# A hybrid decoder layer on one core: products of ones at the start, modulation products two blocks sooner, and the first k/v products taken in fours of blocks

## The chip, the cores and the metric

The kernel runs on one core of a Trainium2 chip. The metric is the device time of one execution in microseconds (us), median of several runs; lower is better. TensorE (PE) does the matrix products, VectorE (DVE), ScalarE (ACT) and GpSimd (POOL) the elementwise work, and SyncE (SP) issues most of the loads. Each engine takes its instructions in the order in which they are queued on it.

## The reference

One layer, 1024 positions by 1024 features, in float32. Only its start matters here:

```python
c_act = jax.nn.silu(c)
mod = c_act @ w_ada + b_ada                       # 6 x 1024 columns
sh1, sc1, g1, sh2, sc2, g2 = jnp.split(mod, 6, axis=-1)
h = rms_norm(x, pre_mix_g) * (1.0 + sc1) + sh1    # 1024 x 1024
proj = h @ w_in                                   # q, k, v and gates of two head groups
...                                               # mLSTM heads, windowed attention, w_out, gated MLP with convolution
```

## The kernel before

The positions are cut into 8 blocks of 128 (`b`), the features into 8 chunks of 128 (`k`), and most of the kernel works on transposed data: `xT[:, k, :]` holds chunk `k` of the normalized `x` for all positions. A product in float32 accuracy is made of three products of parts: each operand is split into a rounded part `hi` (a cast on ACT) and a remainder `lo` (a subtraction on DVE), and hi·hi, hi·lo and lo·hi are summed in PSUM.

**The front.** Everything from the first load to the end of the first projection stands inside `tc.manual_schedule()` (line 201), so that each engine there keeps the order in which the code is written; a planner orders most of what comes behind. The front has these steps:

- SP loads, in this order: the eight blocks of `x` (512 KB each), between them the constants and the first columns of `w_ada` (`ada_pair`, 512 KB a tile), then halves of the first two weight units (`first_load`), then more of `w_ada`.
- For each block, `x_square` (ACT, sum of squares), `rstd_of` (POOL, two small instructions), then `x_turn` (line 265): DVE scales the block by its reciprocal norm, and PE transposes it in eight 128x128 pieces into two PSUM banks, half 0 (tag `mm`, two buffers) and half 1 (tag `B`, two buffers). `x_evac(b, h, ...)` copies a bank into `xT`, on ACT (`C_`) or DVE (`D_`).
- The row of `c` is spread over all partitions by eight products with a slice of the identity (`cb`, line 305), which stand ahead of the first transposes on PE.
- Modulation of chunk 0 comes from PE: `ada_product(8)` and `ada_product(0)` are eight products each with a one-column moving operand (line 320). They stand on PE behind the transposes of block 5 and of block 6. Modulation of the other chunks comes from DVE: `ada_sum` (line 168) multiplies a 128x1024 tile by `cb` and sums it, two of them to a chunk; `shift_gain` makes the shift and the gain from the two sums.
- `h_part(k, t)` returns the four steps that make chunk `k` of `h` for half `t` of the positions (blocks 4t to 4t+3): the affine step on ACT [0] or on DVE [1], the cast to `hi` on ACT [2], the remainder `lo` on DVE [3]. `first_split(u, i)` returns the same two steps, cast and remainder, for half `i` of weight unit `u`.
- The first projection (line 418) runs over the chunks; in each, 16 accumulators (8 blocks, for k/v of attention, `kv`, and for half of the mLSTM values, `v`) take three products of 256 columns, 384 in all. `h_chunk(k)` issues the work for chunk `k + 1` ahead of chunk `k`'s products.

Behind line 334, before the change, the order on the engines is: affine step, cast, remainder of `h` chunk 0, first half, with the split of unit 0 between; the copies of blocks 6 and 7; the split of unit 1; the second half of `h` chunk 0; and then both sums of chunk 1.

Of the kernel before, what the change touches and what calls it, by code (L numbers as in the profile page):

```python
# [18 lines left out]
P = 128  # L19
D = 1024  # L20
S = 1024
NB = S // P
KD = D // P
# [34 lines left out]
def layer_kernel(  # L58
# [18 lines left out]
    V, A, G, T = nc.vector, nc.scalar, nc.gpsimd, nc.tensor  # L77

    def f(ap):
        return ap.bitcast(F32)  # L80
# [7 lines left out]
    def mm3(ps, lh, ll, rh, rl, first, last):  # L88
        T.matmul(ps, lh, rh, start=first, stop=False)  # L89
        T.matmul(ps, lh, rl, start=False, stop=False)  # L90
        return T.matmul(ps, ll, rh, start=False, stop=last)  # L91

    def rstd_of(dst, ssq, n):
        G.tensor_scalar(dst, ssq, 1.0 / n, EPS, op0=ALU.mult, op1=ALU.add)  # L94
        G.tensor_tensor(dst, dst, neghalf[:, : dst.shape[1]], op=ALU.pow)
# [7 lines left out]
    ones = cp.tile([P, P], F32, name="ones")  # L103
# [22 lines left out]
    pC = lambda name: py.tile([P, 512], F32, tag="C", bufs=2, name=name)  # L126
# [4 lines left out]
    def transposed_pair(i, name):  # L131
        return tuple(hp.tile([P, KD, 512], F32R, tag=f"{part}{i}", name=f"{name}{part}{i}") for part in ("hi", "lo"))
# [30 lines left out]
    def ada_load(j, w):  # L163
        nc.sync.dma_start(w, w_ada[j * P : (j + 1) * P, :])
        return w

    def ada_sum(j, w):
        return V.scalar_tensor_tensor(w, w, 0.5, cb, op0=ALU.mult, op1=ALU.mult, accum_out=mod[:, j : j + 1])  # L168
# [19 lines left out]
    units = []  # L188
# [14 lines left out]
    hT = [transposed_pair(i, "hT") for i in range(2)]  # L203
# [5 lines left out]
    def x_load(b):  # L209
        nc.sync.dma_start(xs[b], x[b * P : (b + 1) * P, :])  # L210

    def ada_tile(i, j):
        i = i if i < 10 else (i - 10) ^ 1
        if i < 2:
            return ap0.tile([P, D], F32, tag=f"w{i}", name=f"ada{j}")
        return block_tile(i - 2, f"ada{j}")[:, :D]
# [3 lines left out]
    def ada_pair(k, which=(0, 1)):  # L220
        for i in which:
            j = (8 + k, k)[i]
            adas[j] = ada_load(j, ada_tile(2 * k + i, j))
# [3 lines left out]
    def first_load(u, i):  # L227
        if len(first) <= u:
            raw = w_raw(f"w{u}raw")
            units.append(w_pair(f"w{u}"))  # L230
            first.append((raw, *units[u]))
        c = slice(512 * i, 512 * (i + 1))
        nc.sync.dma_start(first[u][0][:, c], w_in[u][:, c])

    def first_split(u, i):
        raw, hi, lo = (t[:, 512 * i : 512 * (i + 1)] for t in first[u])
        return lambda: A.copy(hi, raw), lambda: V.tensor_tensor(lo, raw, f(hi), op=ALU.subtract)

    nc.scalar.dma_start(ch8, c.rearrange("o (k m) -> (o k) m", k=KD))
    nc.scalar.dma_start(cc8, ccol)  # L240
    x_load(0)
# [3 lines left out]
    nc.sync.dma_start(cv, cols)  # L245
    ada_pair(0, (0,))
    x_load(6)
    x_load(7)
    ada_pair(0, (1,))
    first_load(0, 0)  # L250
    first_load(1, 0)
    ada_pair(1)
# [6 lines left out]
    def x_square(b):  # L259
        A.activation(hT[1][1][:, 6:8, :], xs[b].rearrange("p (a b) -> p a b", a=2), AF.Square, accum_out=ssq[:, b : b + 1])  # L260
        rstd_of(rst[:, b : b + 1], ssq[:, b : b + 1], D)
# [3 lines left out]
    def x_turn(b):  # L265
        V.tensor_scalar(xs[b], xs[b], rst[:, b : b + 1], None, op0=ALU.mult)
        for h in range(2):
            ps = xps[b, h] = (mm, pB)[h](f"xtp{b}")
            for i in range(4):
                T.transpose(ps[:, i * P : (i + 1) * P], xs[b][:, (4 * h + i) * P : (4 * h + i + 1) * P], ident)  # L270

    def x_evac(b, h, copy):
        copy(xT[:, 4 * h : 4 * h + 4, b * P : (b + 1) * P], xps[b, h].rearrange("p (a b) -> p a b", a=4))

    def shift_gain(k):
        c = slice(k, k + 1)
        V.tensor_tensor(mod[:, c], mod[:, c], cv[:, C_BADA + k : C_BADA + k + 1], op=ALU.add)
        V.scalar_tensor_tensor(g_mix[:, c], mod[:, 8 + k : 9 + k], cv[:, C_PREMIX + k : C_PREMIX + k + 1], gb[:, c], op0=ALU.mult, op1=ALU.add)

    def h_part(k, t):  # L280

        c = slice(k, k + 1)
        hk = xT[:, k, 512 * t : 512 * (t + 1)]
        hi, lo = (part[:, k, :] for part in hT[t])
        return (
            lambda: A.activation(hk, hk, AF.Identity, bias=mod[:, c], scale=g_mix[:, c]),
            lambda: V.tensor_scalar(hk, hk, g_mix[:, c], mod[:, c], op0=ALU.mult, op1=ALU.add),
            lambda: A.copy(hi, hk),
            lambda: V.tensor_tensor(lo, hk, f(hi), op=ALU.subtract),
        )  # L290

    C_, D_ = A.copy, V.tensor_copy
# [8 lines left out]
    for h in range(2):  # L301
        cbs.append((mm, pB)[h](f"cb{h}"))
        for i in range(4):
            k = 4 * h + i
# [10 lines left out]
    def ada_product(j):  # L315

        if not mps:
            mps.append(pA("mod0"))
        for k in range(KD):
            T.matmul(mps[0][:, j : j + 1], adas[j][:, k * P : (k + 1) * P], cc8[:, k : k + 1], start=k == 0, stop=k == KD - 1)  # L320

    for b in range(2, NB):
        x_turn(b)
        if b + 1 < NB:
            x_square(b + 1)
        x_evac(b - 2, 0, C_)
        x_evac(b - 1, 1, D_ if b < 6 else C_)
        if b == 5:

            V.scalar_tensor_tensor(gb, cv[:, C_BADA + 8 : C_BADA + 16], 1.0, cv[:, C_PREMIX : C_PREMIX + 8], op0=ALU.add, op1=ALU.mult)  # L330
            ada_product(8)
        if b == 6:
            ada_product(0)
    V.tensor_tensor(mod[:, 0:1], mps[0][:, 0:1], cv[:, C_BADA : C_BADA + 1], op=ALU.add)
    V.scalar_tensor_tensor(g_mix[:, 0:1], mps[0][:, 8:9], cv[:, C_PREMIX : C_PREMIX + 1], gb[:, 0:1], op0=ALU.mult, op1=ALU.add)
    h0, h1 = h_part(0, 0), h_part(0, 1)
    w0, w1 = first_split(0, 0), first_split(1, 0)
    h0[1]()
    w0[0]()
    h0[2]()  # L340
    w0[1]()
    h0[3]()
    x_evac(6, 0, C_)
    x_evac(7, 0, D_)
    w1[0]()
    w1[1]()
    h1[1]()
    h1[2]()
    h1[3]()
    x_evac(7, 1, C_)  # L350

    def ada_sums(k):
        for j in (8 + k, k):
            ada_sum(j, adas[j])
            yield
        shift_gain(k)

    for _ in ada_sums(1):
        pass

    def h_chunk(k):

        if k and k + 3 < KD:
            ada_pair(k + 3)
        sums = ada_sums(k + 2) if k + 2 < KD else iter(())
        if k + 1 < KD:
            for t in range(2):
                act, _, cast, rest = h_part(k + 1, t)
                act()
                cast()  # L370
                next(sums, None)
                rest()
        next(sums, None)
        if k == 0:
            for u in range(2):
                for do in first_split(u, 1):
                    do()
        ensure({1: 3, 3: 4}.get(k, 0))
# [32 lines left out]
    pkv = [p(f"kv{i}") for i in range(2) for p in (pA, pC)]  # L411
    pv = [p(f"v{i}") for i in range(2) for p in (mm, pB)]
    def passes(k):
        if k == 0:
            return [(n, b) for t in range(2) for n in range(2) for b in range(4 * t, 4 * t + 4)]
        return [(n, b) for n in ((0, 1) if k < KD - 1 else (1, 0)) for b in range(NB)]

    for k in range(KD):
        h_chunk(k)
        for n, b in passes(k):  # L420
                hi, lo = hT[b // 4]
                ts = slice((b % 4) * P, (b % 4 + 1) * P)
                uh, ul = (part[:, (k % 4) * 256 : (k % 4 + 1) * 256] for part in units[2 * (k // 4) + n])
                ps = (pkv, pv)[n][b // 2][:, 256 * (b % 2) : 256 * (b % 2 + 1)]

                mm3(ps, hi[:, k, ts], lo[:, k, ts], uh, ul, k == 0 and b % 2 == 0, k == KD - 1 and b % 2 == 1)
    V.tensor_scalar(nsink, rw[:, 8:16], -1.0, None, op0=ALU.mult)
    front.__exit__(None, None, None)
    ap0.release()
# [375 lines left out]
    for h in range(ML_H):  # L805
# [4 lines left out]
        k = conv_chunk(u, 4 + h, f"k{h}")  # L810
# [151 lines left out]
    for b in range(NB):  # L962
# [24 lines left out]
        ts = slice((b % 4) * P, (b % 4 + 1) * P)  # L987
        for h in range(2):
            ps = mm(f"ht{b}_{h}")
# [3 lines left out]
            for i in range(4):  # L993
                k = 4 * h + i
# [154 lines left out]
    units = [(i, r) for i in (1, 2, 6, 5, 7, 3, 4) for r in range(NP)]  # L1149
# [134 lines left out]
    for tb in range(4):  # L1284
        b = 4 + tb
# [101 lines left out]
```

## Time and profile before

| | |
|---|---|
| median of 3 runs | 1127.9 us (1127.55 to 1128.68) |
| the profiled execution | 1128.73 us, of which its span is 1126.7 |
| PE busy | 1110.8 us, 99% of the span, 5949 matmul instructions |
| DVE, ACT, POOL busy | 846.0, 563.2, 150.3 us |
| moved by DMA | 146.85 MB, 130 GB/s on average |

The span runs from the first to the last instruction of the profiled execution; the time holds 2.03 us more. Busy time of an engine is an average over stages, so the table says which engine carries the kernel and not what the first 40 us wait for. The profile also gives the TensorE clock that the chip granted, as a share of 2.4 GHz; its record begins with the first change of level, and what comes before that is shown as 1.00.

### The profile page before, as it was taken

What the parts mean: (1) busy time and instruction counts of PE and PEld (TensorE: products, weight loads), DVE (VectorE), ACT (ScalarE), POOL (GpSimd) and SP (SyncE); (2) the same over time, 40 slices, a digit from 0 to 9 for tenths busy, and PEclk for the clock granted to TensorE, in tenths of its full rate; (3) what the DMA queues carried; (4) which work ended last, traced back from release to release, by engine and by line L of the source; (5) the groups of instructions that cost most, each with busy time, mean ns of one, the idle gap of its engine ahead of it and who ended that gap; (6) DMA issues with size and microseconds to landing.
All of it is one profiled execution on the core that took longest, in us unless ns stands there. A gap on an engine that the chain in (4) does not pass through costs nothing.

```text
span 1126.7 us, 16175 instructions
## 1 busy us (share of the span) xinstructions
PE 1110.8 (99%) x5949; PEld 943.7 (84%) x5949; DVE 846.0 (75%) x1510; ACT 563.2 (50%) x1133; POOL 150.3 (13%) x227
## 2 busy tenths in 40 slices
PE   7999999999999999999999999999999999999997
PEld 6999998888899888877788888888888888888886
DVE  4946879857665456798897888879787877777686
ACT  6642534655535345575553545445454555454552
POOL 2012334554334100000000000000000000000021
PEclk8999999999999999999999999999999999999999
DMA  9625526242103222323333233233313359633445
GB/s 355 236 96 178 166 77 188 94 150 75 38 20 108 100 93 94 113 79 127 103 122 111 67 122 107 72 102 122 121 56 113 132 182 359 230 116 103 150 127 210
DMA packets 55166, 146.85 MB, mean 130 GB/s; under 512 B 5464, under 2 KB 5808, under 8 KB 55088
## 3 DMA queue, kind: packets, MB, share of 16 engines
q1 hardware_dynamic: 53056, 140.31, 37.2%
q10 hardware_dynamic: 2032, 5.51, 1.2%
q8 instruction: 47, 0.77, 0.3%
q14 instruction: 31, 0.25, 0.1%
HBM read 117.19 MB, written 28.61 MB: 129 GB/s over the span
## 4 chain that ended last, share of the span: by engine, by line
PE 90%; DVE 5%; ACT 2%; DMA 2%; issue 1%; POOL 0%; DVEq 0%; POOLq 0%; ACTq 0%
PE X L1036 7%; PE X L1035 7%; PE X L1037 7%; PE Y L1036 4%; PE Y L1037 4%; PE Y L1035 4%; PE dx L1217 3%; PE dx L1215 3%; PE dx L1216 3%; PE tg L89 3%; PE tg L90 3%; PE tg L91 3%; PE dz L1217 3%; PE dz L1216 3%; PE dz L1215 3%; PE y L89 3%
## 5 line engine op out<-in xcount | busy, mean ns | idle before, releaser
L94 POOL TENSOR_SCALAR rsb<-ssb 128x1 f32<-128x1 f32 x4 | 2.3, 576 | 606.8 <-ACT junk L1270 606.6
L1035 PE MATMUL X<-S,wl 128*128 128x512 f32 x156 | 62.5, 400 | 0.0
L1037 PE MATMUL X<-S,wl 128*128 128x512 f32 x156 | 61.7, 396 | 0.0
L1036 PE MATMUL X<-S,wl 128*128 128x512 f32 x156 | 61.6, 395 | 0.0
L1045 DVE SCALAR_TENSOR_TENSOR yg<-ug,cv,yg 128x1023 f32<-128x1023 f32 (+1 forms) x44 | 56.4, 1282 | 6.6 <-ACT yg L1042 6.6
L168 DVE SCALAR_TENSOR_TENSOR ada<-ada,cb 128x1024 f32<-128x1024 f32 x46 | 57.0, 1248 | 3.0 <-DMA ada<-in_w_ada_dram 3.0
L86 ACT CAST wl<-T 128x512 fp32r<-128x512 f32 x41 | 25.5, 622 | 66.1 <-PE X L1036 62.2
L1045 DVE SCALAR_TENSOR_TENSOR yv<-uv,cv,yv 128x1023 f32<-128x1023 f32 (+1 forms) x44 | 56.3, 1279 | 1.2 <-ACT yv L1042 1.2
L86 ACT CAST A<-ra 128x512 fp32r<-128x512 f32 x46 | 28.6, 621 | 49.4 <-PE dx L1217 20.1
L86 ACT CAST w<-T 128x512 fp32r<-128x512 f32 x47 | 29.1, 622 | 40.8 <-PE Z L1037 34.8
L1089 DVE TENSOR_TENSOR uv<-q,X 128x512 f32<-128x512 f32 x22 | 15.1, 687 | 41.3 <-PE X L1037 41.3
L86 DVE TENSOR_TENSOR w<-T,w 128x512 fp32r<-128x512 f32 x47 | 32.2, 689 | 15.4 <-ACT w L86 15.4
L86 DVE TENSOR_TENSOR A<-ra,A 128x512 fp32r<-128x512 f32 x46 | 31.8, 690 | 15.3 <-ACT A L86 15.3
L1217 PE MATMUL dx<-B,A 128*128 128x512 f32 x108 | 42.4, 393 | 0.0
L1216 PE MATMUL dx<-B,A 128*128 128x512 f32 x108 | 42.3, 391 | 0.0
L1215 PE MATMUL dx<-B,A 128*128 128x512 f32 x108 | 39.8, 394 | 0.0
L1037 PE MATMUL Y<-S,wl 128*128 128x512 f32 x92 | 36.4, 395 | 0.0
L1035 PE MATMUL Y<-S,wl 128*128 128x512 f32 x92 | 36.4, 395 | 0.0
L1036 PE MATMUL Y<-S,wl 128*128 128x512 f32 x92 | 36.4, 395 | 0.0
L86 ACT CAST wl<-fu 128x512 fp32r<-128x512 f32 x21 | 13.1, 622 | 46.3 <-PE Y L1036 43.4
L1036 PEld LDWEIGHTS X<-S,wl 128*128 128x128 f32 x156 | 29.3, 188 | 7.4 <-issue 0.5
L1035 PEld LDWEIGHTS X<-S,wl 128*128 128x128 f32 x156 | 29.3, 188 | 7.4 <-issue 0.5
(587 smaller groups left out, 3910.9 us busy)
## 6 DMA issues: line engine op xcount, KB each, us to landing
ada<-in_w_ada_dram SPq DMA_DIRECT2D x48, 512.0 KB, 4.2
ra<-a_dram SPq DMA_DIRECT2D x30, 512.0 KB, 3.9
fu<-in_w_up_dram SPq DMA_DIRECT2D x26, 512.0 KB, 3.5
a_dram<-yg SPq DMA_DIRECT2D x22, 512.0 KB, 3.7
rb<-in_w_down_dram SPq DMA_DIRECT2D x44, 256.0 KB, 4.4
fu_False<-in_w_up_dram SPq DMA_DIRECT2D x18, 512.0 KB, 3.5
a_dram<-s SPq DMA_DIRECT2D x11, 512.0 KB, 5.6
x<-in_x_dram SPq DMA_DIRECT2D x8, 512.0 KB, 7.5
```

Source lines behind the costliest of these rows:

```text
L86: return A.copy(hi, src), eng.tensor_tensor(lo, src, f(hi), op=ALU.subtract)
L89: T.matmul(ps, lh, rh, start=first, stop=False)
L90: T.matmul(ps, lh, rl, start=False, stop=False)
L91: return T.matmul(ps, ll, rh, start=False, stop=last)
L168: return V.scalar_tensor_tensor(w, w, 0.5, cb, op0=ALU.mult, op1=ALU.mult, accum_out=mod[:, j : j + 1])
L1035: T.matmul(ps, w[:, 0, ks], a[:, 0, k, :], start=st, stop=False, skip_group_check=True)
L1036: T.matmul(ps, w[:, 0, ks], a[:, 1, k, :], start=False, stop=False, skip_group_check=True)
L1037: ends = T.matmul(ps, w[:, 1, ks], a[:, 0, k, :], start=False, stop=en, skip_group_check=True)
L1045: V.scalar_tensor_tensor(t[:, sh:], src[:, : S - sh], w(tap), t[:, sh:], op0=ALU.mult, op1=ALU.add)
L1215: T.matmul(ps[tb], a[:, 0, ts], w[:, 0], start=first and r == 0, stop=False, skip_group_check=True)
L1216: T.matmul(ps[tb], a[:, 0, ts], w[:, 1], start=False, stop=False, skip_group_check=True)
L1217: ends = T.matmul(ps[tb], a[:, 1, ts], w[:, 0], start=False, stop=last and r == NP - 1, skip_group_check=True)
```

## The change

Five edits, all in the front:

1. Ahead of everything else, PE gets 12 products of the 128x128 tile `ones` with itself into a PSUM tile that nobody reads.
2. `ada_product(8)` moves from behind block 5's transposes to behind block 4's, `ada_product(0)` from behind block 6's to behind block 5's, and the load of the second one's weights goes ahead of the load of block 7.
3. The split of unit 0 moves into the loop over the blocks (iteration 6); the copy of block 6, half 1, moves out of the loop.
4. Behind the loop the order is new: one sum of chunk 1 stands between the two remainders of chunk 0 that it used to follow, the other ahead of the last remainder, and the copies of blocks 6 and 7 are all on ACT.
5. In the first projection, four accumulators at a time take their hi·hi products, then their hi·lo, then their lo·hi, where before each accumulator took its three in a row.

```diff
+    warm = pC("warm")
+    for i in range(12):
+        T.matmul(warm[:, :P], ones, ones, start=True, stop=True)
     nc.scalar.dma_start(ch8, c.rearrange("o (k m) -> (o k) m", k=KD))
...
     ada_pair(0, (0,))
     x_load(6)
+    ada_pair(0, (1,))
     x_load(7)
-    ada_pair(0, (1,))
     first_load(0, 0)
...
+    w0, w1 = first_split(0, 0), first_split(1, 0)
     for b in range(2, NB):
         x_turn(b)
         if b + 1 < NB:
             x_square(b + 1)
+        if b == NB - 2:
+            w0[0]()
+            w0[1]()
         x_evac(b - 2, 0, C_)
-        x_evac(b - 1, 1, D_ if b < 6 else C_)
+        if b < NB - 1:
+            x_evac(b - 1, 1, D_ if b < 6 else C_)
+        if b == 4:
+            V.scalar_tensor_tensor(gb, cv[:, C_BADA + 8 : C_BADA + 16], 1.0, cv[:, C_PREMIX : C_PREMIX + 8], op0=ALU.add, op1=ALU.mult)
+        if b == 4:
+            ada_product(8)
         if b == 5:
-            V.scalar_tensor_tensor(gb, cv[:, C_BADA + 8 : C_BADA + 16], 1.0, cv[:, C_PREMIX : C_PREMIX + 8], op0=ALU.add, op1=ALU.mult)
-            ada_product(8)
-        if b == 6:
             ada_product(0)
...
     h0, h1 = h_part(0, 0), h_part(0, 1)
-    w0, w1 = first_split(0, 0), first_split(1, 0)
-    h0[1]()
-    w0[0]()
-    h0[2]()
-    w0[1]()
-    h0[3]()
-    x_evac(6, 0, C_)
-    x_evac(7, 0, D_)
-    w1[0]()
-    w1[1]()
-    h1[1]()
-    h1[2]()
-    h1[3]()
-    x_evac(7, 1, C_)
...
-    for _ in ada_sums(1):
+    sums1 = ada_sums(1)
+    h0[1]()
+    h0[2]()
+    next(sums1)
+    h0[3]()
+    w1[0]()
+    w1[1]()
+    x_evac(6, 0, C_)
+    x_evac(7, 0, C_)
+    h1[1]()
+    x_evac(6, 1, C_)
+    h1[2]()
+    for _ in sums1:
         pass
+    h1[3]()
+    x_evac(7, 1, C_)
...
     for k in range(KD):
         h_chunk(k)
-        for n, b in passes(k):
-                hi, lo = hT[b // 4]
-                ts = slice((b % 4) * P, (b % 4 + 1) * P)
-                uh, ul = (part[:, (k % 4) * 256 : (k % 4 + 1) * 256] for part in units[2 * (k // 4) + n])
-                ps = (pkv, pv)[n][b // 2][:, 256 * (b % 2) : 256 * (b % 2 + 1)]
-                mm3(ps, hi[:, k, ts], lo[:, k, ts], uh, ul, k == 0 and b % 2 == 0, k == KD - 1 and b % 2 == 1)
+        todo = passes(k)
+        for i in range(0, len(todo), 4):
+            for term in range(3):
+                for n, b in todo[i : i + 4]:
+                    h_ = hT[b // 4][term == 2][:, k, (b % 4) * P : (b % 4 + 1) * P]
+                    w_ = units[2 * (k // 4) + n][term == 1][:, (k % 4) * 256 : (k % 4 + 1) * 256]
+                    ps = (pkv, pv)[n][b // 2][:, 256 * (b % 2) : 256 * (b % 2 + 1)]
+                    T.matmul(ps, h_, w_, start=k == 0 and term == 0 and b % 2 == 0, stop=k == KD - 1 and term == 2 and b % 2 == 1)
```

## Rows read from the trace of the kernel before

**Rows 1.** The page: busy time of the engines, granted clock in 40 slices.

```profile
PE 1110.8 (99%) x5949; PEld 943.7 (84%) x5949; DVE 846.0 (75%) x1510; ACT 563.2 (50%) x1133; POOL 150.3 (13%) x227
...
PEclk8999999999999999999999999999999999999999
```

**Rows 2.** Stretches (us): length, busy us and instructions by engine, clock, DMA share, GB/s.

```profile
10.10:15.40 5.30, 5.30 (x26) 4.96 (x26) 3.46 (x5) 5.30 (x13) 3.08 (x6) 1.00 1.03 412
...
18.80:22.20 3.40, 3.40 (x34) 3.40 (x32) 1.50 (x4) 1.79 (x5) 1.23 (x2) 1.00 1.04 418
22.20:26.40 4.20, 4.20 (x21) 3.96 (x21) 1.44 (x5) 1.55 (x4) 0.00 (x0) 0.51 0.99 391
26.40:29.10 2.70, 2.70 (x12) 2.46 (x12) 2.34 (x4) 1.23 (x3) 0.00 (x0) 0.50 1.01 395
29.10:33.60 4.50, 4.50 (x39) 4.45 (x38) 4.08 (x8) 1.61 (x3) 0.00 (x0) 1.00 1.00 401
...
200.00:1119.90 919.90, 918.78 (x4430) 761.40 (x4429) 696.56 (x1120) 465.95 (x896) 94.70 (x117) 1.00 0.35 118
```

**Rows 3.** Timeline of PE: start, duration, line, out<-in, count, idle before and releaser.

```profile
6.32 3.78 PE L305 MATMUL cb<-ch,ident 8*128 8x128 f32 x16 [6.32 <-DVE ch L296]
10.03 6.38 PE L270 MATMUL xtp<-ident,x 128*128 128x128 f32 x32
17.02 1.06 PE L270 MATMUL xtp<-ident,x 128*128 128x128 f32 x8 [0.61 <-DVE x L266]
...
19.18 1.84 PE L320 MATMUL mod<-cc,ada 128*128 128x1 f32 x16
...
21.79 2.96 PE L320 MATMUL mod<-cc,ada 128*128 128x1 f32 x16
24.61 1.95 PE L270 MATMUL xtp<-ident,x 128*128 128x128 f32 x8
26.42 0.58 PE L89 MATMUL kv<-w0hi,hThi 128*128 128x256 f32 x1
...
33.48 0.28 PE L91 MATMUL v<-w1hi,hTlo 128*128 128x256 f32 x1
34.34 0.38 PE L89 MATMUL kv<-w0hi,hThi 128*128 128x256 f32 x1 [0.59 <-ACT hThi L288]
...
37.04 0.28 PE L89 MATMUL kv<-w0hi,hThi 128*128 128x256 f32 x1
...
75.19 0.28 PE L89 MATMUL tg<-w4hi,hThi 128*128 128x264 f32 x1
```

**Rows 4.** The chain that ended last, 10 to 37 us, one piece of PE.

```profile
10.10 5.39 PE xtp L270 x24
```

**Rows 5.** Timeline of ACT in the front.

```profile
12.35 0.58 ACT L273 COPY xT<-xtp 128x512 f32<-128x512 f32 x1
...
17.68 1.06 ACT L260 ACTIVATE hTlo<-x 128x1024 fp32r<-128x1024 f32 x1
...
25.74 0.62 ACT L288 CAST hThi<-xT 128x512 fp32r<-128x512 f32 x1 [2.65 <-DVE xT L287]
```

**Rows 6.** Timeline of DVE in the front.

```profile
0.88 0.17 DVE L160 MEMSET ones<- 128x128 f32 x1 [0.88 <-PEq L1376]
...
15.52 0.69 DVE L273 COPY xT<-xtp 128x512 f32<-128x512 f32 x1 [0.42 <-PE xtp L270]
...
20.26 0.75 DVE L266 TENSOR_SCALAR x<-x,rst 128x1024 f32<-128x1024 f32 x1 [0.71 <-POOL rst L95]
24.79 0.16 DVE L334 TENSOR_TENSOR mod<-mod,cv 128x1 f32<-128x1 f32 x1 [3.77 <-PE mod L320]
...
30.09 1.22 DVE L168 SCALAR_TENSOR_TENSOR ada<-ada,cb 128x1024 f32<-128x1024 f32 x1
```

**Rows 7.** SP's issue of the load of `ada0`.

```profile
9.24 0.33 SPq L164 DMA_DIRECT2D ada<-in_w_ada_dram  x1
```

**Rows 8.** Loads issued from 9 to 10 us: size, us from issue to landing.

```profile
ada<-in_w_ada_dram SPq DMA_DIRECT2D x1, 512.0 KB, 9.4
```

## The prediction

> **What bounds the kernel now.** The page comes first: PE is busy for 99% of the span and every other engine for 75% or less [rows 1]. Stretches of the whole span then show where PE isn't: 1.1 us are lost between 200 and 1119.9 us [rows 2]. So behind the front there is no slack, and a front that hands over earlier should move the end by as much. What the front is worth is read from PE's timeline [rows 3]: the first k/v product starts at 26.42 us, the 384 of them end where the next unit's products start, at 75.19, and that is 48.8 us. Undisturbed they need less: the product at 37.04 is the 64th, so the last 321 take 38.15 us, 0.119 each, and 384 would take 45.6. Of the 3.15 us between, 1.5 lie in chunk 0 (48 products from 26.42 to 33.60, 7.2 us where 5.7 would do) and 1.65 in the first 15 products of chunk 1 (33.60 to 37.04). The first loss is the clock: from 22.2 to 29.1 us it was granted at about 0.5, the 1.2 GHz level, and 12 products took 2.7 us [rows 2]. The second is a wait for ACT [rows 3], and the chain behind it runs through DVE, where two sums of 1.22 us start at 30.09 [rows 6].
>
> So the time has two handles: K, the start of the first k/v product, and E, the excess over 45.6 us behind it. Before, K = 26.42 and E = 3.15.
>
> What sets K is PE's order. From 17.02 on PE has hardly a gap: blocks 4 and 5, product 8, block 6, product 0, block 7 [rows 3]. The clock matters here too. The granted level reads 1.00 until 22 us, but that is no measurement: 24 transposes from 10.10 on took 225 ns each [rows 4], eight from 17.02 on 133 ns with their tail [rows 3], so PE was at the low level until about 15.4. A block of eight transposes costs 1.8 us at the low level and 0.95 at the high one; a modulation product costs 1.8 to 3.0 us [rows 3]. PE was at the high level from 15.4, with blocks 3, 4 and 5; it then ran product 8, block 6 and the start of product 0, and at 22.2 the level had fallen.
>
> **The change part by part.** *Products of ones.* The tile is set at 1.05 us [rows 6], and PE had nothing before 6.32. Twelve products are 24 records like `cb`'s 16, which took 236 ns each [rows 3]: 5.7 us, so PE is free at 6.8 at worst, 0.4 late. If the level rises underway they end sooner, and `cb` takes 16 x 0.115 = 1.8 us (a record of a product at the high level) in place of 3.8. Either way this reaches K only in part: block 2 can't be transposed before block 0's bank is copied, and ACT does that at 12.35 to 12.93, behind its squares [rows 5]. PE would start block 2 at 12.9, where it started at 13.7 (10.10 and two blocks of 1.8). After 6.8 us PE has `cb` and two blocks with gaps between, so I take the low level at 12.9, as before.
>
> *Blocks 2 to 4.* Block 2 runs to 14.7. The level rises near 15.4, as before, and block 3 ends at 16.0. Block 4's scaling stands on DVE behind the copy of block 2's second half, which waited for PE at 15.52 before [rows 6] and now follows block 2: 14.7, 15.4, and 0.75 more is 16.15. Block 4 is done at 17.1, 1.0 earlier than before (17.02 + 1.06).
>
> *Products two blocks sooner.* Product 8 runs 17.1 to 18.9, block 5 to 19.9 or 20.7, product 0 to 21.6 (all high) or 23.6 (low from 18.9). Call this moment M; before it was 24.77. The mixture that preceded the fall, products with one column and few transposes, now starts at 17.1 in place of 19.2, so I expect the fall inside it, and take M = 22.8. Blocks 6 and 7 follow: 0.95 to 1.8 each. K is 23.5 (all high), 27.2 (all low), and 26.2 as the value taken, with both blocks mostly low.
>
> The loads trade places: `ada0`'s load was issued at 9.24 and landed 9.4 us later [rows 7, 8], so block 7 lands at 18.6. ACT squared it at 17.68 before [rows 5]; now at 18.7, one us later. Before, POOL's result and the scaling (20.26, 0.75 long) came 2.6 us behind the square's start [rows 5, 6], so block 7 is scaled at 22.0, and PE wants it no sooner than 22.5. That cover is gone only if K were below 23. The other loads keep their places.
>
> *Unit 0's split in the loop.* Cast and remainder, 0.6 and 0.7 us, leave the path between M and K. On DVE the remainder waits for the cast, the cast for ACT's square of block 7 until 19.8; the scaling of block 7 stands behind it and isn't due before 21.2. On ACT the copy of block 4's first half waits until 20.9 at latest, and block 6 needs that bank only at 21.6. I cost this at nothing.
>
> *Order behind M.* On DVE before, from 24.79 to the last of chunk 1's gain (32.7) there were 7.9 us. Now it is the gain (0.3), affine step (0.55), sum (1.22), two remainders (1.3), affine step (0.55), sum (1.22) and gain (0.2): 5.3 us. Chunk 1's first half is then ready on ACT (0.8 and a cast of 0.62 [rows 5]) at M + 6.8, and chunk 0's products don't end before K + 5.7, at least M + 7.6. The 1.65 us of chunk 1 vanish. New waits: the first `lo` is ready at M + 2.8, due eight products behind K, at M + 2.9 at the earliest; the second is ready at M + 6.1, due at M + 5.7 if K = M + 1.9, so at most 0.4 us. The copy of block 6, half 1, now ends at M + 3.6, when `v` of block 2 wants the bank.
>
> *Fours of blocks.* The same 384 products, each with its own weight load as before: PE and PEld count 5949 each [rows 1]. Before, a new accumulator began with every third product, at the same pace of 0.119, so the switch is free.
>
> **Sum.** E is 0.3 (three low products at 0.21 in place of 0.12) and 0.4 (the wait): 0.7. The last k/v product ends at 26.2 + 45.6 + 0.7 = 72.5, 2.7 us before 75.19. The profiled execution took 1128.73 us, 0.83 above the median; from its own time the sum is 1126.0, from the median 1125.2.
>
> **The rivals.** *High throughout*, the clock never falls after block 3. For it: PE has fewer gaps than before. Against: the same products preceded the fall at 22.2 [rows 2, 3]. K = 23.5, E = 0.4, end at 69.5: 1122.2.
>
> *Low into the k/v products*, the level returning 2.7 us behind K as it did before (26.42 to 29.1). For it: K comes behind few dense transposes. K = 27.2, E = 1.9, end at 74.7: 1127.4, no change.
>
> *Given back later*: something behind the front that follows a load or the planner's order keeps its time. Against: PE's 99%. It would read 1127.9.
>
> *Low from the first blocks to K*, the slower one. If the level never rises between 12.9 and K, blocks 2 to 4 end at 18.3, product 8 at 21.3, block 5 at 23.1, product 0 at 26.1, blocks 6 and 7 at 29.7. With E = 1.5 that ends at 76.8 (1129.5); with chunk 0 wholly low (48 x 0.094 = 4.5) at 79.8 (1132.5). It decides if the level hasn't risen by the end of block 4 (18.3) and doesn't rise in blocks 6 and 7 either. Against it stands what happened before: the level rose at 15.4 when PE had done nothing but transposes for 5.3 us [rows 2, 4]. The Trainium skill says otherwise (TensorE: Matmul & The Clock Gate, Part 4: PE-mode transpose): the full-speed clock doesn't engage for transposes, since they don't count as a busy PE. By that rule this rival would be the forecast, 1129.5 to 1132.5; the trace disagrees with it at 15.4, if these are that kind of transpose.
>
> **How the numbers follow.** A time within 0.2% (2.3 us) is what this kernel's measurement can't tell from no change. The likeliest case, a gain of 1.8 to 4.0 us, has 0.53, and about an eighth of it lies within 0.2%; high throughout 0.13; low into the k/v products 0.18; given back 0.10; low from the first blocks 0.06, nearly all of it slower. So faster 0.60, same 0.35, slower 0.05. The predicted time is 1125.2 us. The range reaches from just above the high case to just past the low one: 1122.8 to 1127.7.
>
> **What the profile after would show.** PE's records of ones at 1.1 us and `cb` at 0.115 us a record; block 2 at 12.9; product 8 done by 19; M between 21.6 and 23.6; the first k/v product at 23.5 to 27.2; no wait at chunk 1; the next unit's products at 72.5. The prediction is wrong if the level's fall and rise lie elsewhere than I put them, above all if the first k/v products run at 0.21 us for long, or if PE gains idle time behind 75 us.

## The result, and the profile after

The changed kernel takes 1121.67 us (median of 4 runs, 1120.36 to 1123.5) against 1127.75 for the kernel before on the same chip: a ratio of 0.9946 with a 95% interval of 0.9928 to 0.9963, so 6.1 us or 0.54% faster. The forecast was faster, at 1125.2 and no lower than 1122.8; the gain was more than twice the one predicted. Executions of one kernel differ by up to 5 us here. One execution each of behind_only and before_wide, for the latter the profiled one, ran at a clock of 0.85 and is left out.

The profiled execution took 1121.05 us, its span 1119.2. The timeline of PE, columns as in [rows 3]:

```profile
1.10 4.57 PE L242 MATMUL warm<-ones 128*128 128x128 f32 x24 [1.10 <-DVE neghalf L161]
6.14 2.15 PE L309 MATMUL cb<-ch,ident 8*128 8x128 f32 x16 [0.47 <-DVE ch L300]
8.22 3.48 PE L274 MATMUL xtp<-ident,x 128*128 128x128 f32 x16
11.86 1.09 PE L274 MATMUL xtp<-ident,x 128*128 128x128 f32 x8 [0.17 <-ACT xT L277]
...
14.91 1.09 PE L274 MATMUL xtp<-ident,x 128*128 128x128 f32 x8 [0.43 <-ACT xT L277]
15.84 1.84 PE L324 MATMUL mod<-cc,ada 128*128 128x1 f32 x16
17.55 1.07 PE L274 MATMUL xtp<-ident,x 128*128 128x128 f32 x8
18.45 1.84 PE L324 MATMUL mod<-cc,ada 128*128 128x1 f32 x16
20.16 1.94 PE L274 MATMUL xtp<-ident,x 128*128 128x128 f32 x16
22.15 0.75 PE L440 MATMUL kv<-w0hi,hThi 128*128 128x256 f32 x4
...
68.18 0.28 PE L89 MATMUL tg<-w4hi,hThi 128*128 128x264 f32 x1
```

Both modulation products now take 1.84 us, where the second took 2.96 before, and the last two blocks take 1.94 us together, where the last alone took 1.95 [rows 3]. K is 22.15 (26.42 before), and the next unit starts at 68.18 (75.19 before): 7.0 us sooner, of which 4.3 are K and 2.7 are E, which fell from 3.15 to 0.43 (68.18 - 22.15 - 45.6). The stretches, columns as in [rows 2], give the reason:

```profile
8.00:11.40 3.40, 3.40 (x17) 3.12 (x16) 1.93 (x3) 3.23 (x7) 0.84 (x3) 0.51 1.03 409
11.40:15.84 4.44, 3.41 (x28) 2.70 (x26) 4.12 (x8) 4.29 (x8) 2.25 (x6) 1.00 1.03 414
15.84:20.30 4.46, 4.46 (x43) 4.46 (x42) 2.69 (x5) 3.53 (x9) 1.49 (x4) 1.00 1.03 404
20.30:22.15 1.85, 1.80 (x17) 1.56 (x16) 1.81 (x5) 1.06 (x3) 0.00 (x0) 1.00 1.04 403
22.15:28.31 6.16, 6.16 (x48) 5.97 (x49) 6.12 (x14) 5.59 (x10) 0.00 (x0) 1.00 1.01 395
```

The clock went back to the low level from 8 to 11.4 us, which delayed little (PE still waited for ACT's copies ahead of blocks 2 and 4, 0.17 and 0.43 us), and was at the high one in both products, in blocks 5 to 7 and in the k/v products. DVE's part, columns as in [rows 6]:

```profile
20.52 0.15 DVE L345 TENSOR_TENSOR mod<-mod,cv 128x1 f32<-128x1 f32 x1
...
21.30 1.22 DVE L168 SCALAR_TENSOR_TENSOR ada<-ada,cb 128x1024 f32<-128x1024 f32 x1
...
24.11 1.22 DVE L168 SCALAR_TENSOR_TENSOR ada<-ada,cb 128x1024 f32<-128x1024 f32 x1
...
25.44 0.21 DVE L282 SCALAR_TENSOR_TENSOR gains<-mod,cv,gb 128x1 f32<-128x1 f32 x1
25.57 0.68 DVE L293 TENSOR_TENSOR hTlo<-xT,hThi 128x512 fp32r<-128x512 f32 x1
```

From M to chunk 1's gain it is 5.1 us (20.52 to 25.65), where it was 7.9, and PE runs from chunk 0 into chunk 1 without a wait.

### The profile page after: what moved, and what is told of

Its sections match the earlier page's. It is cut to its first block, busy times and chain, and to the rows that moved or that the text cites. A ratio compares the mean times of both kernels' runs of the same rounds, so it can differ in the third digit from the quotient of the medians.

```text
span 1119.2 us, 16222 instructions
## 1 busy us (share of the span) xinstructions
PE 1108.7 (99%) x5973; PEld 942.3 (84%) x5973; DVE 844.9 (75%) x1509; ACT 563.4 (50%) x1134; POOL 147.0 (13%) x227
## 4 chain that ended last, share of the span: by engine, by line
PE 93%; DVE 2%; DMA 2%; ACT 1%; issue 1%; POOL 0%; SPq 0%; DVEq 0%; POOLq 0%; ACTq 0%
PE X L1050 7%; PE X L1049 7%; PE X L1051 7%; PE Y L1050 4%; PE Y L1051 4%; PE Y L1049 4%; PE dx L1231 3%; PE dx L1229 3%; PE dx L1230 3%; PE tg L89 3%; PE tg L90 3%; PE tg L91 3%; PE dz L1231 3%; PE dz L1229 3%; PE dz L1230 3%; PE y L89 3%
```

## The experiments

| kernel | median us (range, runs) | ratio to before (95%) | next unit starts, us |
|---|---|---|---|
| after_again | 1121.60 (1120.58 to 1124.61, 5) | 0.9950 (0.9937 to 0.9963) | 68.9 |
| no_ones | 1124.12 (1121.65 to 1126.64, 10) | 0.9970 (0.9958 to 0.9981) | 69.2 |
| products_back | 1123.68 (1122.98 to 1127.2, 9) | 0.9972 (0.9962 to 0.9982) | 70.5 |
| order_back | 1125.73 (1123.91 to 1127.93, 11) | 0.9984 (0.9975 to 0.9993) | 72.3 |
| threes | 1124.66 (1122.82 to 1125.41, 6) | 0.9969 (0.9955 to 0.9982) | 71.9 |
| ones_only | 1126.66 (1125.26 to 1128.42, 11) | 0.9994 (0.9985 to 1.0003) | 73.7 |
| behind_only | 1126.11 (1125.28 to 1127.82, 11) | 0.9986 (0.9977 to 0.9996) | 71.1 |
| before_again | 1127.12 (1126.74 to 1129.96, 8) | 0.9994 (0.9984 to 1.0004) | 73.7 |
| before_wide | 1128.38 (1126.5 to 1129.57, 11) | 0.9997 (0.9988 to 1.0006) | |
| wide | 1121.23 (1120.55 to 1121.85, 5) | 0.9944 (0.9931 to 0.9956) | 68.0 |
| wide_threes | 1122.80 (1121.23 to 1123.1, 5) | 0.9955 (0.9942 to 0.9969) | 68.8 |
| wide_no_ones | 1122.75 (1122.31 to 1123.68, 6) | 0.9951 (0.9936 to 0.9965) | 70.2 |
| wide_products_back | 1122.59 (1121.66 to 1123.41, 6) | 0.9949 (0.9936 to 0.9963) | 69.3 |
| wide_sums_late | 1122.67 (1122.14 to 1124.0, 6) | 0.9952 (0.9939 to 0.9966) | 70.7 |
| wide_order_back | 1124.93 (1124.0 to 1125.34, 5) | 0.9966 (0.9953 to 0.9978) | 72.1 |
| wide_cb_dve | 1122.08 (1120.32 to 1123.69, 5) | 0.9941 (0.9928 to 0.9953) | 67.9 |

The groups ran on different occasions, so kernels of different groups are compared by their ratios; 0.001 is 1.1 us. The last column is from one profile each. What follows the next unit's start took between 1050.6 us (ones_only) and 1053.7 us (before_again) in the 17 profiles, so this column alone doesn't order the kernels by time.

**One part undone, or one part alone.** no_ones drops the 12 products; ones_only adds them to the kernel before:

```diff
-    warm = pC("warm")
-    for i in range(12):
-        T.matmul(warm[:, :P], ones, ones, start=True, stop=True)
```

> The changed kernel without its 12 products of ones. Theory A (the ones keep PE at its high clock early, so that blocks 0 to 4 are done sooner and the clock doesn't fall later): cb takes 3.8 us again, M and the first k/v product come 1 to 3 us later than in the changed kernel, 1123 to 1125 us. Theory B (the gain is the new order behind the loads; PE's early clock reaches nothing because ACT and DVE set the pace of blocks 0 to 3): within 0.5 us of the changed kernel's 1121.7.

> The kernel before with the 12 products of ones and nothing else. Theory A: 1.5 to 3 us faster than before, 1125 to 1126.3, since PE's chain from block 4 to the first k/v product starts up to 1 us sooner and more of it runs at the high clock. Theory B: 1127.8, no change; the wait at chunk 1 behind the two sums stays at about 1.5 us.

Without the ones the kernel is 2.7 us slower (0.9970 against 0.9946); alone they give 0.7, an interval that touches no change. The first is within theory A's range; the second lies between A and B. The 2.7 us aren't a cost that every execution pays: five runs of no_ones with a mean granted clock of 0.997 to 0.999 took 1121.65 to 1123.95 us, the other five, at 0.995 or 0.996, 1124.29 to 1126.64.

order_back puts the old block behind the loop back, with unit 0's split in it; threes the old order of terms:

```diff
-        if b == NB - 2:
-
-            w0[0]()
-            w0[1]()
...
-    sums1 = ada_sums(1)
     h0[1]()
+    w0[0]()
     h0[2]()
-    next(sums1)
+    w0[1]()
     h0[3]()
...
+    for _ in ada_sums(1):
+        pass
```

```diff
-            for term in range(3):
-                for n, b in todo[i : i + 4]:
...
+        for n, b in passes(k):
+            mm3(ps, hi[:, k, ts], lo[:, k, ts], uh, ul, ...)
```

> The changed kernel with the old order behind the loop and unit 0's split back there (edits 3 and 4 undone). If the order behind M is worth what the prediction gave it, the wait at chunk 1 returns (1.65 us before) and grows a little because PE arrives sooner: 1123.5 to 1125. If the clock alone made the gain: 1121.7 to 1122.2.

> The changed kernel with the old order of terms: each accumulator takes its three products in a row. Theory: the remainder of h, which now waits behind a sum of 1.22 us on DVE, is due two products behind the first k/v product in place of eight, so PE waits about 0.6 to 1.2 us at the first half and as much at the second: 1122.5 to 1124. Rival: the terms' order only changes where PE waits, not when the remainders are ready, and chunk 0's products end at the same time: 1121.7.

Both cost more than expected, 4.3 and 2.6 us, though the interval of threes overlaps with the changed kernel's. But the trace of threes shows no wait at the k/v products. Its PE timeline:

```profile
15.23 1.84 PE L324 MATMUL mod<-cc,ada 128*128 128x1 f32 x16
16.94 1.59 PE L274 MATMUL xtp<-ident,x 128*128 128x128 f32 x8
18.32 3.41 PE L324 MATMUL mod<-cc,ada 128*128 128x1 f32 x16
21.59 3.65 PE L274 MATMUL xtp<-ident,x 128*128 128x128 f32 x16
24.90 0.56 PE L89 MATMUL kv<-w0hi,hThi 128*128 128x256 f32 x1
```

And its stretches, columns as in [rows 2]:

```profile
17.50:24.90 7.40, 7.40 (x38) 7.40 (x36) 4.45 (x9) 4.55 (x10) 0.74 (x2) 0.50 0.96 376
24.90:27.80 2.90, 2.90 (x16) 2.90 (x15) 2.80 (x8) 2.41 (x5) 0.00 (x0) 0.54 1.01 411
```

Up to its first k/v product threes issues what the changed kernel does. Here the level fell at 17.5, behind product 8, and stayed low into the k/v products: product 0 took 3.41 us in place of 1.84, blocks 6 and 7 3.65 in place of 1.94, and K is 24.90 in place of 22.15. So the fall that I forecast does occur, in some executions, and costs about 3 us of K. The six runs of threes all have a mean granted clock of 0.994 or 0.995. The next runs try to hold the clock, to take it out of the comparison.

**Holding the clock.** after_again is the changed kernel once more. wide gives the moving operand of the modulation products 128 columns, all the same, and reads the first column of each result:

```diff
-            T.matmul(mps[0][:, j : j + 1], adas[j][...], cc8[:, k : k + 1], ...)
+            T.matmul(mps[0][:, 16 * j : 16 * j + P], adas[j][...], cc8[:, k : k + 1].to_broadcast([P, P]), ...)
```

> The changed kernel once more, for a median from more runs on the chip of the next three. If the level of PE's clock between block 4 and the first k/v products differs from run to run, the runs spread over 3 us (1120.4 to 1123.5 so far) and the profile shows one of two pictures: no low stretch behind block 4 and the next unit's products at about 68 us, or a low stretch there and these products 2 to 3 us later. If the spread is of another kind, the profile shows the same clock and other waits.

> The changed kernel with the modulation products 128 columns wide (the moving column repeated 128 times; the first column of each result is read). cb's products show that a record of 128 columns takes 0.115 us at the high level, as a one-column modulation product does, so PE's time at the high level is the same. Theory: the stretch of one-column products is what lets the clock fall; with wide ones it stays high to the end in every run: 1120 to 1121, runs within 1.5 us of each other. Rival: the fall has another cause (transposes, gaps before block 4): the spread of the changed kernel stays, median 1121.7 or, where the products run at the low level and take longer, up to 1123.

The stretches of after_again show yet another picture, low until shortly before the end of block 4 (16.9 us) and high from there:

```profile
10.00:16.75 6.75, 6.46 (x33) 5.86 (x34) 4.47 (x9) 6.59 (x14) 3.34 (x9) 0.56 1.02 410
16.75:21.20 4.45, 4.45 (x43) 4.45 (x42) 3.27 (x5) 3.40 (x7) 1.71 (x4) 1.00 1.05 416
21.20:22.87 1.67, 1.67 (x17) 1.57 (x16) 1.59 (x4) 0.68 (x2) 0.00 (x0) 1.00 1.04 407
```

and PE of wide its products, 16 records in 1.95 us where one-column records took 1.84:

```profile
15.69 1.95 PE L324 MATMUL mod<-cc,ada 128*128 128x128 f32 x16
17.48 1.03 PE L274 MATMUL xtp<-ident,x 128*128 128x128 f32 x8
18.35 1.95 PE L324 MATMUL mod<-cc,ada 128*128 128x128 f32 x16
20.14 1.91 PE L274 MATMUL xtp<-ident,x 128*128 128x128 f32 x16
22.01 0.75 PE L440 MATMUL kv<-w0hi,hThi 128*128 128x256 f32 x4
```

wide's runs lie within 1.3 us; the nine runs of the changed kernel spread over 4.3. Of the ten profiles of kernels with one-column products, the level fell between 17 us and the first k/v products in seven; of the seven with wide products, in none. The kernels of the two groups aren't all the same, but six were run both ways (wide, before_wide and the four below that undo an edit), and the clock of all their runs, 49 against 38, can be compared: its mean is higher with wide products in each of the six, by 0.0014 to 0.0022 (without the ones 0.9988 against 0.9966). In two of the six pairs both kernels ran on the same occasion; the kernel before, which ran on all four occasions, has means of 0.9959 to 0.9963 there. By estimate, 0.0018 of 1122 us at half the clock is 4 us less at the low level in an execution. So it is shown that low stretches are rarer with wide products. Why one comes in a given execution isn't, and wide products don't exclude them: one run of wide_cb_dve took 1123.69 us at a clock of 0.993, and two of wide_products_back 1123.05 at 0.995, without a profile that would show where. The median of wide is 0.4 us below the changed kernel's, less than the runs can tell.

**One part undone with wide products.** products_back puts both products and the second load where they were; wide_products_back, wide_threes, wide_no_ones and wide_order_back are the earlier four with wide products; wide_sums_late moves only the two sums:

```diff
-    next(sums1)
     h0[3]()
...
-    for _ in sums1:
-        pass
     h1[3]()
+    for _ in sums1:
+        pass
```

> The changed kernel with both modulation products and the load of the second one's weights where they were before (edit 2 undone). As the prediction's sum has it, M comes 1 to 2 us later and the first k/v product with it: 1123 to 1124. Rival: PE is without a gap from block 4 on, so the same work ends at the same time in any order and only what stands between M and the first k/v product shows: 1122 to 1122.7.

> wide with both products and the load back (edit 2 undone). Theory: M comes one block later (0.95 us) and PE then waits for ACT's cast ahead of the first k/v product (0.7 us in the profile of products_back): 1.0 to 1.6 us slower than wide, 1122.2 to 1122.8. Rival: the 2 us of products_back were a fall of the clock at the first k/v products, which wide products hold: under 0.7 us.

> The kernel with wide modulation products and the old order of terms (three in a row for each accumulator), to be compared with wide at the same clock. Theory: the first remainder of h is late by 0.6 to 1.2 us and the second by about as much as in wide or more, so 0.6 to 1.5 us slower than wide. Rival: the three us that the old order cost in the changed kernel were the clock's, and at the high clock it costs under 0.3.

> wide without the ones. Theory: at a held clock the ones are worth what the profile of the changed kernel without them showed in the first k/v product, 23.2 against 22.0 to 22.9: 0.4 to 1.2 us slower than wide, 1121.6 to 1122.4. Rival: the ones' 2.4 us are all PE's earlier start, 1123.6.

> The kernel with wide products and the old order behind the loop, unit 0's split included (edits 3 and 4 undone), to be compared with wide at the same clock. The old order cost 4.1 us in the changed kernel, where the profile showed a wait of 1.7 us at chunk 1 and 0.4 at the first k/v product beside a low stretch of the clock. Theory: the order's own share is the waits, 2 to 3.5 us slower than wide (1123.3 to 1124.7), the rest was the clock. Rival: all 4 us are waits, 1125.3.

> wide with both sums of chunk 1 behind the last remainder of chunk 0, all else as in wide (unit 0's split stays in the loop). Theory: chunk 1's gain is ready 2.5 us later, its cast about 1.8 us behind the end of chunk 0's products: 1.5 to 2 us slower than wide, 1122.7 to 1123.2, one wait at chunk 1. Rival: unit 0's split is what the order was worth, and this costs under 0.7 us.

products_back is 2.5 us slower than after_again by the ratios; its profile has the wait for ACT and a low stretch from 23 us. With wide products the wait remains. PE's timeline of wide_products_back, wide_threes, wide_sums_late and wide_order_back, the row at which each waits:

```profile
23.22 0.74 PE L440 MATMUL kv<-w0hi,hThi 128*128 128x256 f32 x4 [0.79 <-ACT hThi L292]
```

```profile
22.92 0.39 PE L91 MATMUL kv<-w0hi,hTlo 128*128 128x256 f32 x1 [0.54 <-DVE hTlo L293]
```

```profile
30.64 0.62 PE L439 MATMUL kv<-w0hi,hThi 128*128 128x256 f32 x3 [1.29 <-ACT hThi L292]
```

```profile
22.55 0.75 PE L435 MATMUL kv<-w0hi,hThi 128*128 128x256 f32 x4 [0.84 <-ACT hThi L292]
...
30.56 0.76 PE L435 MATMUL kv<-w0hi,hThi 128*128 128x256 f32 x4 [1.72 <-ACT hThi L292]
```

The products, the terms and the order each have a wait of their own, at the place the theory named: the products 0.8 us at the first k/v product, the terms 0.5 at the first remainder, the sums 1.3 at chunk 1, unit 0's split and the sums together 0.8 and 1.7. wide_no_ones has none there; its blocks 0 to 3 end at 16.5 us and K is 24.17, and its median lies between its theory (1122.4 at most) and the rival (1123.6). By the medians the single parts cost 1.4 to 1.6 us and the whole order 3.7; by the ratios 0.6 to 1.3 and 2.5. The intervals of the single parts overlap with wide's, so their sizes aren't settled; the places of the waits are.

**The kernel before, again.** before_again is a second profile of it, before_wide has wide products and nothing else, behind_only has edits 3, 4 and 5 alone.

> The kernel before once more, with its own profile. In the trace that the prediction was made from, block 1's square began at 8.0 us and block 3's at 11.3; in the seven traces of the later kernels they began at 6.0 to 6.5 and 9.9 to 10.6. Theory: this is a difference between executions (when the first loads land), so here too they begin at about 6.3 and 10.2, block 4's transposes end about 1 us sooner than 18.1, and the next unit's products come at 73.5 to 74.5. Rival: the changed kernel loads sooner because of something in it; then the picture of the first trace returns, 75.2.

> The kernel before with the modulation products 128 columns wide and nothing else. If the low level of PE's clock from product 0 to the middle of chunk 0 was worth what the prediction took from the rows (2 us ahead of the first k/v product, 1.5 us in chunk 0, less what the DVE chain of sums gives back as a longer wait at chunk 1), the kernel is 1 to 2 us faster, 1125.5 to 1126.7. If the wide products don't hold the clock there: 1127.5, or up to 1128.5 where they run at the low level.

> The kernel before with what stands behind the loads alone (edits 3, 4 and 5: unit 0's split, the order of sums and copies, the terms in fours), without the ones and with the products where they were. If the parts simply add, it keeps 6.0 - 2.4 - 2.0 = 1.6 us of the gain: 1126. If the chain through DVE is what bounds the kernel before and PE's earlier work pays only behind it, this part alone gives more than half: 1124 to 1125. If it needs PE's earlier work, nothing: 1127.5.

PE's timeline of before_again:

```profile
18.77 1.84 PE L320 MATMUL mod<-cc,ada 128*128 128x1 f32 x16
...
21.39 1.84 PE L320 MATMUL mod<-cc,ada 128*128 128x1 f32 x16
23.09 1.07 PE L270 MATMUL xtp<-ident,x 128*128 128x128 f32 x8
```

```profile
24.89 0.46 PE L89 MATMUL kv<-w0hi,hThi 128*128 128x256 f32 x1 [0.73 <-ACT hThi L288]
...
32.82 0.39 PE L89 MATMUL kv<-w0hi,hThi 128*128 128x256 f32 x1 [0.19 <-ACT hThi L288]
```

and of ones_only, product 0 and the first product of chunk 1:

```profile
19.86 3.41 PE L323 MATMUL mod<-cc,ada 128*128 128x1 f32 x16
...
32.87 0.39 PE L89 MATMUL kv<-w0hi,hThi 128*128 128x256 f32 x1
```

The square of block 1 on ACT, in the trace before and in before_again:

```profile
8.02 1.06 ACT L260 ACTIVATE hTlo<-x 128x1024 fp32r<-128x1024 f32 x1 [1.97 <-DMA x<-in_x_dram]
```

```profile
6.01 1.06 ACT L260 ACTIVATE hTlo<-x 128x1024 fp32r<-128x1024 f32 x1 [0.23 <-DMA x<-in_x_dram]
```

So even of the kernel before my one trace showed one case. Here the level fell only at 25 us, block 1's square began at 6.0 in place of 8.0, and K was 24.89 with PE waiting for ACT (block 4 ended at 17.7, only 0.4 us sooner). The next unit starts at 73.68, 1.5 us sooner than in [rows 3]. What decides this is the end of product 0, M: chunk 1's first product, which waits for DVE's sums, starts 9.6 us behind it in all three profiles that have the order of before on DVE and the products in their old places (24.75 and 34.34 before, 23.23 and 32.82 here, 23.27 and 32.87 in ones_only). Chunk 0 ran at the low level for 2.7, 3.4 and 4.2 us of these 9.6, and the wait at chunk 1 was 0.59 us, 0.19 and none. So the kernel before keeps what PE gains ahead of M, and gives back in this wait what it gains in chunk 0. The ones brought block 4 forward, but in ones_only's profile product 0 then ran at the low level, and M came no sooner than here. That before_wide is no faster than before fits this, but no profile shows it. behind_only keeps 1.6 us by its ratio (0.5 to 2.6), as the additive reading had it (6.0 - 2.4 - 2.0 = 1.6).

**An attempt at a faster one.** wide_cb_dve, which also puts block 7's load ahead of `ada0`'s again:

```diff
-        A.copy(cb[:, 512 * h : 512 * (h + 1)], cbs[h])
+        V.tensor_copy(cb[:, 512 * h : 512 * (h + 1)], cbs[h])
```

> An attempt at a faster one: wide products, the two copies of cb on DVE in place of ACT, block 7's load ahead of ada0's again. ACT's squares of blocks 3 to 5 come 1 us sooner, so PE starts its gapless stretch (block 4 to block 7) about 0.8 us sooner, and block 7 lands in time: 0.4 to 1.0 us faster than wide, 1120.2 to 1120.8. Rival: M plus ACT's and DVE's steps sets the first k/v product now, and DVE's longer list delays the blocks' scaling: 1121.2 or more.

It isn't faster than wide by anything the runs can tell. K is 21.87 against 22.01; ACT's squares came sooner, but block 4's transposes still began at 14.69 (14.76 in wide), now behind DVE, which had taken the copies over:

```profile
14.69 1.07 PE L274 MATMUL xtp<-ident,x 128*128 128x128 f32 x8 [0.28 <-DVE x L270]
```

## Why the prediction was wrong, step by step

- *What bounds the kernel* held. Nothing behind the front gave time back: the span behind the next unit's start is 1051.5 us before and 1051.0 after, and E and K account for 7.0 of the 7.5 us between the two spans (by itself weak evidence, as that span varies by 3 us between profiles). Of the forecast gain of 2.7 us nearly all was E's, and E came as forecast (3.15 to 0.43, for 0.7); the miss is K's, 26.2 forecast and 22.15 measured. One reading of E was wrong: the low level in chunk 0 (1.5 us) and the wait behind it (1.65) don't add, since before, in before_again and in ones_only chunk 1 started 9.6 us behind M, however long chunk 0 was low; the change removed both, so the sum wasn't hurt by it.
- *Products of ones*: 24 records in 4.6 us (4.3 to 5.5 in other profiles) for at most 5.7 predicted, cb in 2.15 for 1.8. Held.
- *Blocks 2 to 4*: predicted done at 17.1; 16.0 in the profile after, 16.9 in after_again. I had the low level until 15.4; in the profile after it ended at 11.4, in after_again at about 16. Block 1's square began at 6.0 and 6.5 in these two, against 8.0 in the trace before; before_again has 6.0 without the change, so that part is the execution's.
- *Products two blocks sooner* is the step that failed: "so I expect the fall inside it, and take M = 22.8", and with it "26.2 as the value taken, with both blocks mostly low". The level didn't fall there in either profile of the changed kernel (two of its nine runs, 1123.5 and 1124.61 us, have a mean clock of 0.994, as the profiled run of threes has, but no profile shows where they were low). Products and block 5 took 4.5 us in both, where I had 5.7, and blocks 6 and 7 1.7 to 1.9, where I had 3.4: M is 20.3 and 21.2, K 22.15 and 22.87. That is 2.8 us of K; the rest of the 4 us in the first profile is block 4's earlier end. The rival "high throughout", which I gave 0.13 and 1122.2 us, is what both profiles show.
- The ground for that step was one fall in one trace, read as what the mixture does. threes and the count of profiles show it to be what the mixture does in some executions; I should have given both levels nearly even chances and let the range reach the high case.
- *The second half of the price*: I took the low case at K = 27.2. In threes, low from 17.5 on, K was 24.9. Even the low case was priced too high: block 4 was done at 15.4 where I had 17.1, and product 8 still ran at the high level.
- *Loads, unit 0's split*: nothing, as predicted; block 7's square began at 17.6 and its transposes at 21 had it in time.
- *Order behind M*: 5.1 us for 5.3, no wait at chunk 1, E 0.43 for 0.7. Held; undone with wide products it showed the waits of 0.8 and 1.7 us.
- *Fours of blocks* cost nothing in pace. Their worth, which I left inside the sum, is the wait of 0.5 us that wide_threes shows.
- The slower rival, low from the first blocks to K, appeared in none of the 17 profiles. Where it would have come from the rule of the Trainium skill that transposes don't engage the full clock (TensorE: Matmul & The Clock Gate, Part 4: PE-mode transpose), after_again disagrees once more, if these are that kind of transpose: PE did nothing but transposes from 10.25 to 16.75 us, at a mean of 0.56 from 10.00 on, and was at 1.00 from there.

## What to carry to other kernels

Where a stretch of a timeline can run at either level of PE's clock, one profile shows one draw: take a second profile, or price both, before taking a value. Here a one-column product cost hardly more with 128 equal columns (1.95 us against 1.84 for 16 records), and with those the clock held through that stretch in all seven profiles, while single runs (a clock of 0.993 in one of wide_cb_dve) still had long low stretches. And ask which chain releases the next stage: in the kernel before, what PE gained in chunk 0 couldn't reach the end, because DVE's sums held chunk 1 until M + 9.6 us. The ones alone gave 0.7 us, an interval that touches no change, edits 3 to 5 alone 1.6, all five together 6.1.

## What the runs showed of the hardware that wasn't expected

The level of the clock between 10 and 25 us differed between executions of the same instructions: low from 10 to 16 and high behind (after_again), low from 8 to 11.4 only (the profile after), high to 17.5 and low to 27.8 (threes). With the same loads issued in the same order, block 1 was squared at 6.0 us in one execution of the kernel before and at 8.0 in another.

The level also fell far behind the front, in two of the 17 profiles: from 165.0 to 168.4 us in before_again and from 160.3 to 163.7 in wide_threes. PE was busy throughout and at 1.00 until then, as the stretches of before_again show, and in both it had just run the same products of 65 columns:

```profile
161.60:165.00 3.40, 3.40 (x30) 2.82 (x28) 2.47 (x6) 1.03 (x3) 1.63 (x5) 1.00 0.81 173
165.00:168.40 3.40, 3.40 (x21) 3.17 (x21) 3.00 (x5) 0.38 (x1) 0.29 (x1) 0.50 0.54 177
```

```profile
164.63 0.39 PE L551 MATMUL po<-vat,pT 128*128 128x65 f32 x2
```

The same products ran at 1.00 in the other profiles at an undisturbed clock. That they let the level fall, as the one-column products do, is argued from these two cases and not tested.
